# A new hand-written order for the first stage of a hybrid S5 and attention block, with more of its splitting on ScalarE and small S5 copies on GpSimd

## The chip, the cores and the metric

The kernel runs on one core of one Trainium2 chip. The metric is the device time of one execution in microseconds. Before the change the median of three runs is 1468.1 us (1466.05 to 1469.47).

## What is computed

One decoder block over a sequence of 1024 rows of width 1024, in float32. A vector `c` gives shifts and scales. The first stage of the kernel, which the change rewrites, makes the first shift and scale, the normed and modulated input `h`, its projection `u`, and the constants of the S5 recurrence:

```python
cond = jax.nn.silu(c)
mod = (cond @ w_ada[l] + b_ada[l])[:, None, :]
sh1, sc1, g1, sh2, sc2, g2 = jnp.split(mod, N_ADA, axis=-1)
h = modulate(rmsnorm(x, norm1_g[l]), sh1, sc1)      # h * (1 + scale) + shift
u, q, k, v, gate_a, gate_b = jnp.split(h @ w_in[l], IN_SPLITS, axis=-1)
...
lam_bar = jnp.exp(lam * dt)                          # per group and state
b_bar = ((lam_bar - 1.0) / lam)[..., None] * b
_, states = lax.associative_scan(_linear_recurrence, (a, bu), axis=1)
y = jnp.einsum('btgp,gip->btgi', states, cmat).real + d_skip * uf
```

The rest (stick-breaking attention, gates, output projection, SwiGLU) is not touched.

## The kernel before

Every float32 product is made of three products of shorter numbers. An operand is split in a high part (a copy that rounds, float32 to fp32r) and a low part (what is left), and TensorE multiplies high by high, low by high and high by low. So each `h` tile needs a high part and a low part before its products can run: tile `pa` or `pb`, `[:, 0]` high and `[:, 1]` low.

`start()` (from L560) is the first stage. It stands under a manual schedule: on all five engines its instructions run in the order in which the code issues them. What follows it (S5 proper, the value and gate projections, glu) is ordered by a scheduler that plays the program against a timeline of its own; so a change in `start()` also moves instructions behind it.

The stage, in its order:

- `x` comes in eight tiles of 128 rows, four for each half of the sequence (`load`). Each row gets its sum of squares (`squares`, tiles `sqa` on ScalarE and `sqv` on VectorE), then 1/rms (`rstd`, L481 to L487), and is scaled by it (`scale`, L637 and L639).
- `turn(h, k)` (L644) transposes 128 columns of the four scaled tiles of half `h` into a PSUM tile `tp`, of which there are two.
- `ada_products(g)` (L978, copied out at L611 into `acc`) and `ada_sums(g)` (L617) make shift and scale for 256 columns; VectorE finishes them as `mod` (L620) and `G` (L621).
- `modulate(h, k)` makes the split `h` tile: ScalarE writes the high part straight from PSUM (L648), VectorE computes the same value in float32 (`hf`, L650) and subtracts (L651).
- `product(h, ks, ms)` (L657) multiplies by `w_in`, split in `u_split` (L592, L593). There are 12 products of 512 columns for each `k` and half, 192 in all. `store(h, m)` (L661, L662) copies the sums out, on ScalarE for even `m` and on VectorE for odd `m`, and writes them to DRAM, from where the S5 stage reads them again as `u`.
- `S5.steps()` is a generator of the S5 constants, six pieces of small VectorE instructions (L85 to L168), which the stage calls between its own work. `S5.matrices()` (L185) ends the stage: `b_bar` (L73 to L78, `bbr` and `bbi`), twelve copies into `bst`, `A` and `B` (L202 to L207), eight transposes of `cl` on TensorE (L213) with two copies by ScalarE, and one of `dsk` (L217).

The order is: half 0 in four groups `g` of two `k` each (the last group of the first half is `g` = 3, tiles `u3h` and `u3l`), then half 1. The squares and scaling of half 1 stand in group 2, ahead of the copy L611 of group 3's sums. Each engine's instructions start in the order in which they stand.

Behind the stage VectorE builds the S5 matrices (`o<-C,A` L276, `scr<-Cs,B` L275, `e` L73 to L78 from copies L242 and L243 on ScalarE, `tc`/`tn`) while TensorE makes the values (L770) and gates (L749), whose weights need a low part from VectorE (`wl`, `wgl`, L455).

Of the kernel before, what the change touches and what calls it, by code (L numbers as in the profile page):

```python
# [9 lines left out]
F32 = mybir.dt.float32  # L10
# [18 lines left out]
class S5:  # L29
# [53 lines left out]
    def steps(self):  # L83
# [29 lines left out]
        for k in (11, 9, 7, 5, 3):  # L113
            stt(s, s, (-1) ** (k // 2) / math.factorial(k), w, ALU.add, ALU.mult)
        stt(s, s, 1.0, ph, ALU.add, ALU.mult)
        ts(c, w, -1.0 / math.factorial(14), None, ALU.mult)
        for k in (12, 10, 8, 6, 4, 2):
# [67 lines left out]
    def matrices(self):  # L185
        nc, pool, work = self.nc, self.pool, self.work
        v = nc.vector
        ts = v.tensor_scalar
        br, bi, zr, zi, lpr, lpi = self.br, self.bi, self.zr, self.zi, self.lpr, self.lpi
# [9 lines left out]
        for g in range(2):  # L199
            h = slice(64 * g, 64 * g + 64)  # L200
            lo, hi = slice(0, 64), slice(64, 128)
            v.tensor_copy(bst[lo, :, g], bbr[h])  # L202
            v.tensor_copy(bst[hi, :, g], bbi[h])
            v.tensor_copy(A[lo, :, g], lpr[h])
            ts(A[hi, :, g], lpr[h], -1.0, None, ALU.mult)
            ts(B[lo, :, g], lpi[h], -1.0, None, ALU.mult)
            ts(B[hi, :, g], lpi[h], -1.0, None, ALU.mult)  # L207
        self.C = pool.tile([128, 32, 16], F32, name="C")
# [8 lines left out]
        nc.tensor.transpose(ps[0:16, 0:32], self.dsk, self.ident[0:32, 0:32])  # L217
        nc.vector.tensor_copy(self.dT, ps[0:16, 0:32])

# [206 lines left out]
class Block:  # L426
# [132 lines left out]
    def start(self, const, up, s5p):  # L559
# [8 lines left out]
        with self.pool("s0", 1, side="right") as sp, self.pool("s0a", 1, side="right") as ap, self.pool("s5t", 1, side="right") as st, \  # L568
# [53 lines left out]

            def squares(h):
                for t in range(4 * h, 4 * h + 4):
                    if t % 2:
                        sq = ap.tile([P, 1024], F32, name="sqv")
                        nc.vector.scalar_tensor_tensor(sq, x[t], 1.0, x[t], ALU.mult, ALU.mult, accum_out=ss[:, t:t + 1])
                    else:
                        sq = ap.tile([P, 1024], F32, name="sqa")
                        nc.scalar.activation(sq, x[t], AF.Square, accum_out=ss[:, t:t + 1])  # L630

            def scale(h):
                r = self.rstd(const, ss[:, 4 * h:4 * h + 4], 4)
                for t in range(4):
                    xt, rt = x[4 * h + t], r[:, t:t + 1]
                    if t == 0:
                        nc.scalar.mul(xt, xt, rt)  # L637
                    else:
                        nc.vector.tensor_scalar(xt, xt, rt, None, ALU.mult)  # L639

# [5 lines left out]
            def modulate(h, k):  # L646
                t, q = self.hT[h][k], turned[h, k]
                nc.scalar.activation(t[:, 0], q, AF.Identity, bias=mod[:, 0, k:k + 1], scale=G[:, k:k + 1])  # L648
                f = ap.tile([P, 512], F32, name="hf", bufs=2)
                nc.vector.tensor_scalar(f, q, G[:, k:k + 1], mod[:, 0, k:k + 1], ALU.mult, ALU.add)  # L650
                nc.vector.tensor_tensor(t[:, 1], f, t[:, 0].bitcast(F32), ALU.subtract)  # L651
# [7 lines left out]
            def store(h, m):  # L659
                u = up.tile([P, 8, 64], F32, name="us", bufs=4)  # L660
                self.upin = (nc.vector.tensor_copy if m % 2 else nc.scalar.copy)(u, acc[m].rearrange("p (c j) -> p j c", j=8))  # L661
                nc.sync.dma_start(out=self.uD[P * m:P * m + P, :, 64 * h:64 * h + 64], in_=u)  # L662
# [8 lines left out]
            nc.vector.tensor_scalar(self.cond32, self.cond.unsqueeze(2).broadcast_to([P, KT, 32]), 1.0 / 32.0, None, ALU.mult)  # L671
            squares(0)
            scale(0)
            turn(0, 0)
# [6 lines left out]
            steps = s5.steps()  # L681
            next(steps)
            ada_sums(0)
            acc = [(self.mm, mp)[m // 2].tile([P, 512], F32, name="mm") for m in range(4)]
            for g in range(4):
                k = 2 * g
                modulate(0, k)
                modulate(0, k + 1)
                if g < 3:
                    u_split(g + 1)  # L690
                if g == 0:
                    u_load(2)
# [15 lines left out]
                next(steps)  # L708
                ada_sums(g + 1)
                product(0, (k + 1,), range(4))  # L710
            s5.load()
            self.hT[1] = [self.PB.tile([P, 2, 512], F32R, name="pb") for _ in range(KT)]
            product(0, (6,), range(4))
            turn(1, 0)
            modulate(1, 0)
            next(steps)
            for m in range(4):
                if m == 2:
                    turn(1, 1)
                    modulate(1, 1)  # L720
                product(0, (7,), (m,))
                store(0, m)
            acc = [xp.tile([P, 512], F32, name="mm")] + [(self.mm, self.mm, mp)[m].tile([P, 512], F32, name="mm") for m in range(3)]
            for k in range(4):
                turn(1, k + 2)
                product(1, (k,), range(4))
                modulate(1, k + 2)
                if k == 0:
                    next(steps)
            for k in (6, 7):  # L730
                turn(1, k)
                modulate(1, k)
            s5.matrices()
            for m in range(4):
                product(1, range(4, KT), (m,))
                store(1, m)


# [857 lines left out]
```

## Time and profile before

| | before |
|---|---|
| median of three runs | 1468.1 us |
| the profiled execution's own time | 1467.38 us |
| its span | 1465.7 us |
| TensorE busy | 1410.2 us, 96% |
| VectorE busy | 1091.1 us, 74% |
| ScalarE busy | 628.8 us, 43% |
| GpSimd busy | 511.6 us, 35% |

Some 1.7 us of the execution lie outside the span. A row of the timeline reads: start, duration, engine, line, operation, output <- input, and in brackets the idle time of the engine before it with what ended it. A row of the windows reads: the stretch, its length, then busy time and instructions of TensorE (PE), its weight loads, VectorE (DVE), ScalarE (ACT), GpSimd (POOL), the clock that TensorE was granted (1.00 is full), and the DMA share with GB/s. A busy TensorE need not be at its peak.

### The profile page before, as it was taken

What the parts mean: (1) busy time and instruction counts of PE and PEld (TensorE: products, weight loads), DVE (VectorE), ACT (ScalarE), POOL (GpSimd) and SP (SyncE); (2) the same over time, 40 slices, a digit from 0 to 9 for tenths busy, and PEclk for the clock granted to TensorE, in tenths of its full rate; (3) what the DMA queues carried; (4) which work ended last, traced back from release to release, by engine and by line L of the source; (5) the groups of instructions that cost most, each with busy time, mean ns of one, the idle gap of its engine ahead of it and who ended that gap; (6) DMA issues with size and microseconds to landing.
All of it is one profiled execution on the core that took longest, in us unless ns stands there. A gap on an engine that the chain in (4) does not pass through costs nothing.

```text
span 1465.7 us, 18286 instructions
## 1 busy us (share of the span) xinstructions
PE 1410.2 (96%) x6730; PEld 1117.0 (76%) x6730; DVE 1091.1 (74%) x1424; ACT 628.8 (43%) x829; POOL 511.6 (35%) x279
## 2 busy tenths in 40 slices
PE   5898999999899999999999999999999999999997
PEld 3678888788666666667888788888888888788886
DVE  5779996357788889886833679777766666889896
ACT  3321121642586858675418543223233323434334
POOL 1000000001211122102410014886757566689395
PEclk9999999999999999999999999999999999999999
DMA  9545664569211111116452223544434369899722
GB/s 338 142 108 160 155 179 117 180 214 343 89 44 43 37 51 58 51 51 216 143 201 87 86 87 101 182 146 166 148 120 147 122 204 370 293 376 369 246 85 115
DMA packets 193561, 233.39 MB, mean 159 GB/s; under 512 B 29500, under 2 KB 128896, under 8 KB 193472
## 3 DMA queue, kind: packets, MB, share of 16 engines
q1 hardware_dynamic: 184336, 224.70, 46.8%
q10 hardware_dynamic: 8912, 7.48, 1.9%
q8 instruction: 53, 0.87, 0.3%
q14 instruction: 36, 0.29, 0.1%
q0 software_dynamic: 224, 0.05, 0.0%
HBM read 162.85 MB, written 68.16 MB: 158 GB/s over the span
## 4 chain that ended last, share of the span: by engine, by line
PE 76%; DVE 10%; DMA 6%; ACT 5%; issue 2%; SPq 0%; POOL 0%; ACTq 0%; POOLq 0%; DVEq 0%
PE tq L1290 13%; PE wo L1290 6%; PE mm L1290 6%; PE tq L1411 6%; PE mx L823 5%; PE ga L749 4%; PE mm L823 4%; PE wo L1411 3%; PE mm L1411 3%; DMA aw<-in_w_ada_dram 2%; PE acc L823 2%; PE mm L1128 2%; PE mm L657 2%; PE z L823 2%; PE wo L1128 2%
## 5 line engine op out<-in xcount | busy, mean ns | idle before, releaser
L471 POOL TENSOR_TENSOR ws<-wb 128x1024 f32<-128x1024 f32 x24 | 61.6, 2567 | 175.4 <-DVE wl L474 148.7
L455 POOL TENSOR_TENSOR wl<-ws,wh 128x1024 fp32r<-128x1024 f32 x12 | 30.8, 2564 | 163.4 <-ACT wh L452 108.8
L916 DVE TENSOR_TENSOR wa<-wa,acc 128x512 f32<-128x512 f32 (+1 forms) x80 | 47.0, 628 | 32.6 <-ACT row L914 30.2
L294 POOL MEMSET tz<- 128x1024 f32 x4 | 3.8, 953 | 179.8 <-PE mm L657 96.7
L1337 POOL TENSOR_TENSOR pa<-pa 128x512 f32<-128x512 f32 x30 | 63.2, 2135 | 0.3
L1281 POOL TENSOR_TENSOR f<-f,f 128x512 f32<-128x512 f32 x30 | 53.2, 1797 | 24.9 <-DVE f L1275 19.6
L888 ACT ACTIVATE ws<-wa 128x1024 f32<-128x1024 f32 (+1 forms) x40 | 39.0, 976 | 48.6 <-DVE wa L885 48.3
L893 DVE TENSOR_TENSOR wl<-ws,wh 128x1024 fp32r<-128x1024 f32 (+1 forms) x40 | 57.1, 1427 | 1.0
L474 DVE TENSOR_TENSOR wl<-ws,wh 128x1024 fp32r<-128x1024 f32 x23 | 42.0, 1827 | 20.4 <-ACT wh L473 20.4
L993 DVE SCALAR_TENSOR_TENSOR acc<-aw,cond,acc 128x512 f32<-128x512 f32 x56 | 43.9, 784 | 7.0 <-DMA aw<-in_w_ada_dram 6.0
L1366 POOL TENSOR_TENSOR pa<-pa,row 128x1024 f32<-128x1024 f32 x14 | 43.7, 3135 | 14.9 <-DMA pa<-in_w_ffn_down_dram 14.9
L1411 PE MATMUL tq<-f,f 128*128 128x512 f32 x156 | 47.2, 390 | 1.3 <-DVE f L474 1.3
L1274 ACT ACTIVATE f<-f 128x1024 f32<-128x1024 f32 x20 | 21.2, 1061 | 62.1 <-DVE f L1310 31.4
L891 DVE SCALAR_TENSOR_TENSOR ws<-wa,ws 128x1024 f32<-128x1024 f32 (+1 forms) x40 | 45.5, 1136 | 2.9 <-ACT ws L890 1.9
L919 ACT ACTIVATE wa<-wa 128x1024 f32<-128x1024 f32 (+1 forms) x40 | 38.8, 971 | 19.5 <-DVE wa L916 18.5
L452 ACT CAST wh<-ws 128x1024 fp32r<-128x1024 f32 x24 | 25.0, 1049 | 48.6 <-PE wo L1128 23.3
L473 ACT CAST wh<-ws 128x1024 fp32r<-128x1024 f32 x23 | 24.1, 1053 | 50.6 <-PE tq L1290 31.1
L823 PE MATMUL z<-q,k 64*128 64x512 f32 (+3 forms) x192 | 41.8, 526 | 4.0 <-DVE wa L885 2.8
L1290 PE MATMUL tq<-pa,wh 128*128 128x512 f32 x144 | 44.3, 389 | 0.0
L1290 PE MATMUL tq<-x,wh 128*128 128x512 f32 x144 | 44.3, 389 | 0.0
L471 POOL TENSOR_TENSOR wgs<-wb 128x1024 f32<-128x1024 f32 x12 | 28.9, 2407 | 42.0 <-DVE wl L474 21.1
L473 ACT CAST wh<-wb 128x1024 fp32r<-128x1024 f32 x25 | 26.2, 1051 | 40.1 <-PE tq L1290 19.1
(914 smaller groups left out, 4687.0 us busy)
## 6 DMA issues: line engine op xcount, KB each, us to landing
wb<-hD SPq DMA_DIRECT2D x40, 512.0 KB, 6.0
aw<-in_w_ada_dram SPq DMA_DIRECT2D x64, 256.0 KB, 4.4
hD<-f SPq DMA_DIRECT2D x30, 512.0 KB, 5.5
ws<-in_w_in_dram SPq DMA_DIRECT2D x23, 512.0 KB, 4.4
wb<-in_w_ffn_gate_dram SPq DMA_DIRECT2D x44, 256.0 KB, 4.2
wb<-in_w_ffn_up_dram SPq DMA_DIRECT2D x44, 256.0 KB, 4.9
ws<-hD SPq DMA_DIRECT2D x20, 512.0 KB, 6.2
x<-in_x_dram SPq DMA_DIRECT2D x16, 512.0 KB, 7.1
```

Of the source, the lines that this page charges most:

```text
L471: (add or nc.gpsimd).tensor_tensor(st, a, b, op)
L473: nc.scalar.copy(h, a)
L749: self.nc.tensor.matmul(ps, lhsT=w[a][:, k], rhs=act[h][k][:, b], start=(j == 0), stop=(j == n - 1))
L823: return self.tc.keep_in_program_order(self.nc.tensor.matmul(*args, **kw))
L891: nc.vector.scalar_tensor_tensor(st, a, 0.0, st, ALU.max, ALU.add)
L893: nc.vector.tensor_tensor(lt, st, ht.bitcast(F32), ALU.subtract)
L916: nc.vector.tensor_tensor(a[:, x, 0:f], a[:, x, 0:f], r[:, x, 0:f], ALU.subtract)
L1128: self.nc.tensor.matmul(ps, lhsT=mg[t // 4][k][:, a, P * (t % 4):P * (t % 4) + P], rhs=ws[k // 2][b][:, k % 2], start=k + j == 0, stop=k + ...
L1281: self.last_sum = nc.gpsimd.tensor_tensor(o, a, b, op)
L1290: self.nc.tensor.matmul(ps, lhsT=w[x][:, q, k], rhs=self.B[i](y, k), start=(j == 0), stop=(j == 11))
L1337: self.after(nc.gpsimd.tensor_tensor(t[:, n], part(a), part(b), SIGN_B[i]), first)
L1411: nc.tensor.matmul(ps, lhsT=o[x][:, P * t:P * t + P], rhs=o[y][:, R], start=(j == 0), stop=(j == 3 * np_ - 1))
```

## The change

It rewrites the order of `start()` and moves work between engines; the arithmetic stays as it is.

- The squares and the scaling of half 1 are taken apart. Two squares of half 1, one on ScalarE and one on VectorE, now stand ahead of the copy of group 3's sums and two behind it, both on ScalarE; the scaling stands behind group 3's `modulate`.
- `modulate` has a second form, for odd `k` and all of half 1: ScalarE writes the float32 value `hf` from PSUM and then copies it to the high part from SBUF; VectorE only subtracts. Twelve `hf` instructions go from VectorE to ScalarE, and twelve copies of 128x512 are added on ScalarE.
- The S5 steps are cut in eight pieces and called later: the first behind group 0 and not ahead of `ada_sums(0)`, the polynomials for sine and cosine in half 1 and not in group 2.
- Half 1 takes its last two tiles in the loop (`k` up to 5), so only `k` = 6 and 7 are left for the end, where 24 and not 48 products stand.
- The twelve copies into `A`, `B` and `bst` go to GpSimd. The transposes of `cl` and `dsk` come behind the second of the last four products (`turned`); the copy `dT` goes to ScalarE.
- All four sums of half 1 are copied out by ScalarE.
- On the DMA queue the third and fourth `w_in` tiles are loaded behind `w_ada` tiles.

```diff
             def modulate(h, k):
                 t, q = self.hT[h][k], turned[h, k]
-                nc.scalar.activation(t[:, 0], q, AF.Identity, bias=mod[:, 0, k:k + 1], scale=G[:, k:k + 1])
                 f = ap.tile([P, 512], F32, name="hf", bufs=2)
-                nc.vector.tensor_scalar(f, q, G[:, k:k + 1], mod[:, 0, k:k + 1], ALU.mult, ALU.add)
+                if h == 0 and k % 2 == 0:
+                    nc.scalar.activation(t[:, 0], q, AF.Identity, bias=mod[:, 0, k:k + 1], scale=G[:, k:k + 1])
+                    nc.vector.tensor_scalar(f, q, G[:, k:k + 1], mod[:, 0, k:k + 1], ALU.mult, ALU.add)
+                else:
+                    nc.scalar.activation(f, q, AF.Identity, bias=mod[:, 0, k:k + 1], scale=G[:, k:k + 1])
+                    nc.scalar.copy(t[:, 0], f)
                 nc.vector.tensor_tensor(t[:, 1], f, t[:, 0].bitcast(F32), ALU.subtract)
...
-                self.upin = (nc.vector.tensor_copy if m % 2 else nc.scalar.copy)(u, acc[m].rearrange("p (c j) -> p j c", j=8))
+                self.upin = (nc.vector.tensor_copy if m % 2 > h else nc.scalar.copy)(u, acc[m].rearrange("p (c j) -> p j c", j=8))
...
                 if g == 0:
+                    ada_load(2)
                     u_load(2)
-                    ada_load(2)
-                    u_load(3)
                     load(1)
                 if g == 1:
                     ada_load(3)
-                if g == 2:
-                    squares(1)
-                    scale(1)
+                    u_load(3)
                 if g == 3:
                     break
+                if g == 2:
+                    square(4, True)
+                    square(5, False)
                 product(0, (k,), (0, 1))
                 ada_products(g + 1)
...
-                next(steps)
+                if g < 2:
+                    next(steps)
+                if g == 1:
+                    next(steps)
+                if g == 2:
+                    square(6, True)
+                    square(7, True)
+                    next(steps)
+                    r = self.rstd(const, ss[:, 4:8], 4)
                 ada_sums(g + 1)
                 product(0, (k + 1,), range(4))
+            for t in range(4, 8):
+                scale(r, t)
...
-            for k in range(4):
+            for k in range(6):
                 turn(1, k + 2)
                 product(1, (k,), range(4))
                 modulate(1, k + 2)
-                if k == 0:
+                if k < 3 or k == 5:
                     next(steps)
-            for k in (6, 7):
-                turn(1, k)
-                modulate(1, k)
             s5.matrices()
             for m in range(4):
-                product(1, range(4, KT), (m,))
+                product(1, (6, 7), (m,))
                 store(1, m)
+                if m == 1:
+                    s5.turned()
```

In `matrices` the twelve copies change their engine:

```diff
-            v.tensor_copy(bst[lo, :, g], bbr[h])
-            v.tensor_copy(bst[hi, :, g], bbi[h])
-            v.tensor_copy(A[lo, :, g], lpr[h])
...
+            gp.tensor_copy(A[lo, :, g], lpr[h])
+            gp.tensor_scalar(A[hi, :, g], lpr[h], -1.0, None, ALU.mult)
...
+            gp.tensor_copy(bst[lo, :, g], bbr[h])
+            gp.tensor_copy(bst[hi, :, g], bbi[h])
+
+    def turned(self):
```

On ScalarE, at the end of group 2, these rows stood before (`u3h` is the high part of the fourth weight tile, `sqa` a square, `acc` the copy that `ada_sums(3)` waits for, `pa` the high parts of group 3):

```order
L592 CAST u3h<-ws 128x1024
L630 ACTIVATE sqa,ss_108<-x 128x1024 x2
L482 ACTIVATE ry<-rv 128x4
L483 ACTIVATE ry<-ry 128x4
L637 ACTIVATE x<-x,ry 128x1024
L611 COPY acc<-mm 128x512
L648 ACTIVATE pa<-tp,mod_141,G_142 128x512 x2
```

At the same place on ScalarE now:

```order
L596 CAST u3h<-ws 128x1024
L630 ACTIVATE sqa,ss_108<-x 128x1024
L615 COPY acc<-mm 128x512
L630 ACTIVATE sqa,ss_108<-x 128x1024 x2
L486 ACTIVATE ry<-rv 128x4
L487 ACTIVATE ry<-ry 128x4
L649 ACTIVATE pa<-tp,mod_141,G_142 128x512
L652 ACTIVATE hf<-tp,mod_141,G_142 128x512
L653 CAST pa<-hf 128x512
L636 ACTIVATE x<-x,ry 128x1024
```

The copy `acc` has moved ahead of two squares, the 1/rms and the scaling, and the scaling has moved behind the high parts.

On VectorE, where half 0 ends and half 1 begins, these rows stood before (`rho` is the last of the long S5 step, `us` the copies of the sums of half 0, `pb` a low part of half 1):

```order
L147 TENSOR_TENSOR rho<-rho 128x16
L661 COPY us<-mm 128x512
L650 TENSOR_SCALAR hf<-tp,G_142,mod_141 128x512
L651 TENSOR_TENSOR pb<-hf,pb 128x512
L661 COPY us<-mm 128x512
L650 TENSOR_SCALAR hf<-tp,G_142,mod_141 128x512
L651 TENSOR_TENSOR pb<-hf,pb 128x512
```

At the same place on VectorE now (`sa` is the polynomial for the sine):

```order
L638 TENSOR_SCALAR x<-x,ry 128x1024 x3
L654 TENSOR_TENSOR pb<-hf,pb 128x512
L664 COPY us<-mm 128x512
L654 TENSOR_TENSOR pb<-hf,pb 128x512
L664 COPY us<-mm 128x512
L654 TENSOR_TENSOR pb<-hf,pb 128x512
L113 TENSOR_SCALAR sa<-aw 128x128
L115 SCALAR_TENSOR_TENSOR sa<-sa,aw 128x128 x5
```

The copies `us` now stand ahead of all S5 steps of this half, and no `hf` is left here.

On TensorE, at the end of the loop over half 1, these rows stood before (`tp` are transposes, `cl` and `dsk` S5 inputs):

```order
L657 MATMUL mm<-pb,wh 128x512
L644 MATMUL tp<-ident,x 128x128 x8
L213 MATMUL tp<-ident,cl 128x128 x8
L217 MATMUL tp<-ident,dsk 16x32
L657 MATMUL mm<-pb,wgh 128x512
L657 MATMUL mm<-pb,wgl 128x512
```

The same transposes on TensorE now (the rows of L781 are the first value products, which the scheduler puts here; the last 12 products of L660 follow later):

```order
L660 MATMUL mm<-pb,u3l 128x512
L660 MATMUL mm<-pb,u3h 128x512
L217 MATMUL tp<-ident,cl 128x128 x8
L781 MATMUL mm<-wh,pa 128x256
L781 MATMUL mm<-wl,pa 128x256
L781 MATMUL mm<-wh,pa 128x256 x2
```

The 17 transposes in a row are gone: two turns have moved into the loop, and those of `cl` stand behind products.

More of the change, by code (lines that the diff above doesn't have):

```diff
@@ L93, in steps @@
         self.vexp(r, ar, tmp)
+        yield
         def reduce(n, th):
@@ L115, in steps @@
         stt(s, s, 1.0, ph, ALU.add, ALU.mult)
+        yield
         ts(c, w, -1.0 / math.factorial(14), None, ALU.mult)
@@ L201, in matrices @@
             lo, hi = slice(0, 64), slice(64, 128)
[L202 to L207 removed]
+            gp.tensor_copy(A[lo, :, g], lpr[h])
+            gp.tensor_scalar(A[hi, :, g], lpr[h], -1.0, None, ALU.mult)
+            gp.tensor_scalar(B[lo, :, g], lpi[h], -1.0, None, ALU.mult)
+            gp.tensor_scalar(B[hi, :, g], lpi[h], -1.0, None, ALU.mult)
+            gp.tensor_copy(bst[lo, :, g], bbr[h])
+            gp.tensor_copy(bst[hi, :, g], bbi[h])
+    def turned(self):
+        nc, pool = self.nc, self.pool
         self.C = pool.tile([128, 32, 16], F32, name="C")
@@ L217, in matrices @@
         nc.tensor.transpose(ps[0:16, 0:32], self.dsk, self.ident[0:32, 0:32])
-        nc.vector.tensor_copy(self.dT, ps[0:16, 0:32])
+        nc.scalar.copy(self.dT, ps[0:16, 0:32])
     def phases(self):
@@ L621, in ada_sums, with square, scale @@
                 nc.vector.scalar_tensor_tensor(G[:, s], mod[:, 1, s], 1.0, self.cols[:, 48 + 2 * g:50 + 2 * g], ALU.add, ALU.mult)
[L623 to L639, printed above, removed]
+            def square(t, act):
+                sq = ap.tile([P, 1024], F32, name="sqa" if act else "sqv")
+                if act:
+                    nc.scalar.activation(sq, x[t], AF.Square, accum_out=ss[:, t:t + 1])
+                else:
+                    nc.vector.scalar_tensor_tensor(sq, x[t], 1.0, x[t], ALU.mult, ALU.mult, accum_out=ss[:, t:t + 1])
+            def scale(r, t):
+                if t % 4 == 0:
+                    nc.scalar.mul(x[t], x[t], r[:, t % 4:t % 4 + 1])
+                else:
+                    nc.vector.tensor_scalar(x[t], x[t], r[:, t % 4:t % 4 + 1], None, ALU.mult)
             def turn(h, k):
@@ L671, in start @@
             nc.vector.tensor_scalar(self.cond32, self.cond.unsqueeze(2).broadcast_to([P, KT, 32]), 1.0 / 32.0, None, ALU.mult)
-            squares(0)
-            scale(0)
+            acc = [(self.mm, mp)[m // 2].tile([P, 512], F32, name="mm") for m in range(4)]
+            for t in range(4):
+                square(t, t % 2 == 0)
+            r = self.rstd(const, ss[:, 0:4], 4)
+            for t in range(4):
+                scale(r, t)
             turn(0, 0)
@@ L681, in start @@
             steps = s5.steps()
-            next(steps)
             ada_sums(0)
-            acc = [(self.mm, mp)[m // 2].tile([P, 512], F32, name="mm") for m in range(4)]
             for g in range(4):
@@ L707, in start @@
                 turn(0, k + 3)
-                next(steps)
+                if g < 2:
[7 more added lines that the diff above has]
+                    r = self.rstd(const, ss[:, 4:8], 4)
                 ada_sums(g + 1)
                 product(0, (k + 1,), range(4))
+            for t in range(4, 8):
+                scale(r, t)
             s5.load()
@@ L713, in start @@
             product(0, (6,), range(4))
-            turn(1, 0)
-            modulate(1, 0)
-            next(steps)
             for m in range(4):
-                if m == 2:
-                    turn(1, 1)
-                    modulate(1, 1)
                 product(0, (7,), (m,))
                 store(0, m)
+                if m % 2 == 0:
+                    turn(1, m // 2)
+                    modulate(1, m // 2)
             acc = [xp.tile([P, 512], F32, name="mm")] + [(self.mm, self.mm, mp)[m].tile([P, 512], F32, name="mm") for m in range(3)]
-            for k in range(4):
+            for k in range(6):
                 turn(1, k + 2)
```

4 lines of the change are left out of this document (2 added, 2 removed).

## The prediction

> **What bounds the kernel now.** I read the page first, then the busy time of the engines in windows cut at the stage's own joints, then the timeline at each wait of TensorE.
>
> ```profile
> span 1465.7 us, 18286 instructions
> ...
> PE 1410.2 (96%) x6730; PEld 1117.0 (76%) x6730; DVE 1091.1 (74%) x1424; ACT 628.8 (43%) x829; POOL 511.6 (35%) x279
> ```
>
> TensorE is busy nearly throughout, but a busy TensorE includes slow stretches. The windows over the first stage, two stretches inside it, and the S5 stage behind it (length; PE, PEld, DVE, ACT, POOL busy; granted clock; DMA):
>
> ```profile
> 46.70:62.20 15.50, 11.39 (x73) 7.89 (x73) 13.26 (x35) 4.41 (x8) 0.00 (x0) 0.89 0.52 140
> 62.20:82.80 20.60, 18.39 (x93) 14.60 (x92) 16.84 (x59) 6.62 (x9) 0.00 (x0) 1.00 0.34 78
> 82.80:102.20 19.40, 16.47 (x68) 12.89 (x67) 10.40 (x27) 5.81 (x9) 0.00 (x0) 0.82 0.28 65
> 55.70:59.20 3.50, 3.30 (x9) 2.02 (x7) 2.74 (x12) 0.36 (x1) 0.00 (x0) 0.51 0.00 0
> 59.20:61.30 2.10, 0.79 (x3) 0.35 (x3) 1.61 (x3) 1.09 (x2) 0.00 (x0) 1.00 0.00 0
> 86.40:93.20 6.80, 6.12 (x19) 4.40 (x18) 6.62 (x21) 1.17 (x2) 0.00 (x0) 0.50 0.27 77
> 102.20:210.00 107.80, 101.63 (x750) 92.60 (x748) 99.70 (x232) 19.33 (x40) 3.07 (x6) 0.98 0.65 166
> ```
>
> Between 46.7 and 102.2 us TensorE waits, and twice it runs at half clock: 3.5 us from 55.7 and 6.8 us from 86.4. ScalarE is idle for two thirds of this time and VectorE is what TensorE mostly waits for. Here the waits are, with what ended each in brackets:
>
> ```profile
> 53.01 0.57 ACT L611 COPY acc<-mm 128x512 f32<-128x512 f32 x1
> 53.62 1.05 PE L617 MATMUL adap<-ones,acc 128*128 128x1 f32 x8 [2.61 <-ACT acc L611]
> ...
> 71.20 0.50 PE L657 MATMUL mm<-pb,wh 128*128 128x512 f32 x1 [1.88 <-DVE us L661]
> ...
> 82.77 1.03 PE L644 MATMUL tp<-ident,x 128*128 128x128 f32 x8
> ...
> 86.06 0.78 PE L213 MATMUL tp<-ident,cl 128*128 128x128 f32 x4 [2.25 <-DVE hf L650]
> ...
> 87.52 1.12 PE L213 MATMUL tp<-ident,cl 128*128 128x128 f32 x4 [0.68 <-ACT C L214]
> ```
>
> Each of the two half-clock stretches follows one of these waits by about 2 us or less. In the chain of work that ended last, the same product runs at two speeds:
>
> ```profile
> 33.26 4.22 PE mm L657 x18
> ...
> 41.31 0.44 PE tp L644 x4
> 41.74 0.80 PE adap L617 x8
> ...
> 88.78 13.37 PE mm L657 x48
> ```
>
> 18 products in 4.22 us are 0.234 us each; 48 in 13.37 us are 0.279 each. So TensorE bounds the stage only between its waits, and what can be gained is the waits and the slow products. From 102.2 to 210 us VectorE is busy for 99.7 of 107.8 us, so an early TensorE is worth something there only if VectorE is early too.
>
> **The change, part by part.** Up to 46.7 us I cost it at nothing: TensorE's order is unchanged, and an `hf` on VectorE gives way to 0.6 us of ScalarE there. The cover is TensorE's own queue of products in each group; if it were gone, the price would be below 1 us a group.
>
> *Group 3's start (T1).* These rows carry the walk:
>
> ```profile
> 44.36 1.05 ACT L592 CAST u3h<-ws 128x1024 fp32r<-128x1024 f32 x1
> ...
> 46.48 1.06 ACT L630 ACTIVATE sqa<-x 128x1024 f32<-128x1024 f32 x1
> 47.45 0.19 ACT L630 ACTIVATION_READ_ACCUMULATOR sqa<-x 128x1 f32 x1
> ...
> 48.54 0.66 PE L644 MATMUL tp<-ident,x 128*128 128x128 f32 x4
> ...
> 50.48 0.17 DVE L481 TENSOR_SCALAR rv<-ss 128x4 f32<-128x4 f32 x1
> ...
> 51.75 0.16 DVE L487 TENSOR_TENSOR ry<-ry,ra 128x4 f32<-128x4 f32 x1
> ...
> 58.40 0.15 DVE L620 TENSOR_TENSOR mod<-adap,cols 128x4 f32<-128x4 f32 x1
> ...
> 58.84 1.45 ACT L648 ACTIVATE pa<-tp,mod,G 128x512 fp32r<-128x512 f32 x2 [5.27 <-DVE G L621]
> ...
> 61.25 0.73 PE L657 MATMUL mm<-pa,u3h 128*128 128x512 f32 x2 [0.84 <-DVE pa L651]
> ```
>
> The added copies of 128x512 have no row in this stage. The same form stands in the glu stage:
>
> ```profile
> L1027 ACT CAST y2p<-sg x8: 611/620/625, 289.4 to 307.9; 128x512 fp32r<-128x512 f32 x8
> ```
>
> I take 0.62 us for each. ScalarE then starts `u3h` at 44.36 + 0.62 = 45.0 and ends it at 46.0; one square (1.06, and 0.19 to read its sum) ends at 47.2, before TensorE is done with the sums at 48.54. So the copy `acc` starts at 48.6 and not at 53.01, and the wait of 2.61 us goes, and with it, I take it, the half clock behind it. What is late next is the coefficients: two squares on ScalarE (2.3 us) end at 51.5, 1/rms takes 50.48 to 51.91, so 1.4 us, to 53.0, `mod` and `G` 0.44 us (58.40 to 58.84), and `pa` starts at 53.5 and not 58.84. TensorE comes there at 54.5: 48.54 plus two turns of four transposes (0.44 each), six products (1.4), the sums (0.8) and twelve products (2.8). Its first low part is ready 61.25 - 58.84 = 2.4 us behind `pa`, at 55.9 and not 61.25. That is 5.3 us earlier; T1 = 5.2, rounded down.
>
> *Start of half 1 (T2).* The wait of 1.88 us was for a copy `us` that stood on VectorE behind the long S5 step. It now stands ahead of it. T2 = 1.9.
>
> *End of half 1 (T3, T4).* From 82.77 to 88.78 are 6.0 us, in which 17 transposes ran, work for 1.9 us at 0.44 for four. The eight turns wait no more (two sit in the loop; `tp` is freed by ScalarE), and those of `cl` stand behind products. T3 = 6.0 - 1.9 = 4.1, say 4.0. The 48 products at 0.234 take 11.2 us and not 13.37 if no wait slows the clock: T4 = 2.1.
>
> Does VectorE keep up, now that two S5 pieces move into half 1? Rows for its load:
>
> ```profile
> L650 DVE TENSOR_SCALAR hf<-tp,G,mod 128x512 f32<-128x512 f32 x16 | 12.9, 806 | 6.1 <-ACT pa L648 3.6 <-ACT pb L648 2.5
> ...
> 53.95 0.22 DVE L112 TENSOR_SCALAR sa<-aw 128x128 f32<-128x128 f32 x1
> ...
> 58.25 0.23 DVE L119 TENSOR_SCALAR ca<-ca 128x128 f32<-128x128 f32 x1
> ...
> 90.10 0.28 DVE L202 COPY bst<-bbr 64x256 f32<-64x256 f32 x1
> ...
> 93.28 0.18 DVE L218 COPY dT<-tp 16x32 f32<-16x32 f32 x1
> ```
>
> It was busy 16.84 + 10.40 = 27.2 us from 62.2 to 102.2. Eight `hf` (6.4), the twelve copies and `dT` (90.10 to 93.46, 3.4) and a copy `us` (0.7) go; the polynomials (53.95 to 58.48, 4.5) come: 21.2 us. TensorE needs 40.0 - 1.9 - 4.0 - 2.1 = 32 us for the same stretch. The joint that matters is the sixth tile: ahead of its low part VectorE has about the work of 62.2 to 82.8 with six `hf` (4.8) out and the polynomials in, 16.84 - 4.8 + 4.5 = 16.5 us, against five rounds of TensorE of twelve products and a turn, 5 x 3.25 = 16.3 us. They are equal, though the last S5 step of that window now comes later. So I take off 0.3 us for new waits, up to 3 for the range (one tile late by 1 us and a slow clock behind it).
>
> *The GpSimd copies.* No small copy of GpSimd stands in the trace. Its nearest rows:
>
> ```profile
> L294 POOL MEMSET tz<- 128x1024 f32 x4 | 3.8, 953 | 179.8 <-PE mm L657 96.7
> ...
> L471 POOL TENSOR_TENSOR ws<-wb 128x1024 f32<-128x1024 f32 x24 | 61.6, 2567 | 175.4 <-DVE wl L474 148.7
> ```
>
> Four to seven times the elements take 0.95 and 2.57 us, so a copy costs between 0.13 and 2.57 us; I take 0.4, near the memset in elements. Four stand between `bbi` (done at 90.10 before, so about 85 with T1) and the second half of `A`, which `o<-C,A` on VectorE waits for, with all of the S5 work queued behind it: `A` is there at 86.6, at 95 by the upper end. The cover is that VectorE's next work but two needs the copies `e` of ScalarE, which stand behind the last `us`:
>
> ```profile
> 102.18 0.25 ACT L242 COPY e<-bbr 128x64 f32<-128x64 f32 x1 [0.35 <-PE mm L657]
> ...
> 104.97 0.22 DVE L74 TENSOR_TENSOR p<-e,lpi 128x64 f32<-128x64 f32 x1
> ...
> 140.92 0.48 PE L770 MATMUL mm<-wl,pa 128*128 128x256 f32 x1 [4.72 <-DVE wl L455]
> ```
>
> TensorE's last product of the stage comes at 102.2 - 13 = 89 us, or 91 with the value products that now run ahead of it; so `e` comes at 91, `p<-e` at 91.5, and 85 + 4p + 1.4 (two `o` of 0.7) is hidden up to p = 1.3 us a copy. The upper end costs 85 + 10.3 + 1.4 - 91.5 = 5 us. [...]
>
> *Behind the stage (T5).* VectorE and TensorE both enter the S5 stage some 13 us earlier, with the same work. The scheduler has reordered it: the two low parts of which TensorE awaited one for 4.72 us now stand ahead of the widest `tc` products and not behind them. New waits may come; I take 2 of the 4.7 us.
>
> The sum: 5.2 + 1.9 + 4.0 + 2.1 - 0.3 = 12.9 in the stage, 14.9 with T5. The profiled execution took 1467.38 us, 0.7 under the median of 1468.1. I predict 1467.4 - 14.9 = 1452.5.
>
> **The rivals.**
>
> *The lead is spent in the S5 stage.* `e` comes only 102.18 - 91.3 = 11 us earlier, and VectorE with its loads is the bound there (99.7 of 107.8 us). For it: the chain of waits runs over VectorE there. Against: VectorE's own load is not raised. If a late tile costs its 3 us as well and the new order loses 2 us, the gain is 13 - 3 - 2 - 1 = 7: 1460.
>
> *More goes than the waits of the stage.* If the whole 4.72 us goes and as much as 2 us of slow products behind it, the gain is 13 + 6.7: 1447.5.
>
> *GpSimd becomes the bound, slower than before.* If `A` comes so late that VectorE stands still, all S5 work moves. From 85 + 4p + 1.4 = 91.5 + 15 the gain is gone: p = 5.0 us. At p = 6 VectorE is 18.9 us late and the result is 1467.4 + 3.9 = 1471.3. Against: the widest row is 2.57 us for four times the elements.
>
> *The change does not do what it says:* the coefficients of group 3 or a late load hold TensorE as long as `acc` did, and VectorE is late in half 1 by what T2 to T4 give. Then 1467.
>
> *The clock.* A half clock of 3.5 us stood behind the wait of 2.61 us, none in the 2.1 us from 59.2, with two waits. The walk leaves TensorE one wait of about 1.3 us. [...]
>
> **How the numbers follow.** The forecast (1449 to 1457) gets 0.55, the lead spent (1457 to 1464) 0.20, more gone (1442 to 1449) 0.17, GpSimd as the bound 0.04, no effect 0.04. The likeliest is 1452.5. The range reaches over the first three but for their ends, with 3 us of late tile and clock and 5 us of GpSimd on one side and 6.7 us of S5 waits on the other: 1443 to 1462. A measurement of this kernel tells 0.2%, 2.9 us, from no change. Faster by more: 0.92; within: 0.04; slower: 0.04.
>
> **What would show it.** In the profile after: no wait for the copy `acc` in group 3 and `pa` of group 3 at 53 to 54.5 us; clock 1.00 in the stage from 30 us on; the products at 0.234 throughout; the last product of the stage at 88 to 92 us; `o<-C,A` at 86 to 89 us and the first `p<-e` at 91 to 93. It would be wrong if the low part of the sixth tile held TensorE, if small GpSimd copies took over 2 us each, or if TensorE's waits between 100 and 330 us grew by more than 4 us.

## The result, and the profile after

The changed kernel takes 1458.67 us (median of five runs, 1455.89 to 1462.33) against 1468.1. The ratio is 0.9942 with a 95% interval of 0.9921 to 0.9963, so it is 5.4 to 11.6 us faster (8.5 by the ratio, 9.4 by the medians); 14.9 were forecast. Its profiled execution is the longest of the five (1462.33 us) and only 5.1 us shorter than the profiled one of before (1467.38).

The page of the changed kernel:

```profile
span 1460.6 us, 18303 instructions
...
PE 1411.3 (97%) x6730; PEld 1117.7 (77%) x6730; DVE 1081.5 (74%) x1395; ACT 640.1 (44%) x846; POOL 514.7 (35%) x291
```

Its windows over the same places: group 3 with the start of half 1; from the start of group 3's products to the end of the stage, in two pieces; the S5 stage; and its four half-clock stretches ahead of 400 us:

```profile
46.70:62.20 15.50, 14.90 (x101) 11.34 (x100) 10.59 (x33) 9.85 (x18) 0.00 (x0) 1.00 0.58 150
...
56.10:74.90 18.80, 18.80 (x95) 15.52 (x96) 14.26 (x45) 10.84 (x16) 0.00 (x0) 1.00 0.38 85
74.90:91.60 16.70, 16.70 (x95) 14.17 (x94) 10.76 (x41) 8.29 (x14) 6.41 (x13) 1.00 0.39 97
23.30:30.20 6.90, 6.43 (x38) 2.81 (x38) 6.06 (x22) 2.06 (x3) 0.00 (x0) 0.51 1.09 352
91.60:199.40 107.80, 106.87 (x764) 96.33 (x763) 99.51 (x230) 21.55 (x42) 2.66 (x6) 1.00 0.66 175
238.35:241.80 3.45, 3.45 (x19) 3.45 (x18) 0.00 (x0) 0.66 (x2) 0.00 (x0) 0.51 1.09 309
269.00:275.90 6.90, 5.57 (x14) 4.19 (x14) 3.05 (x3) 6.09 (x7) 0.26 (x1) 0.51 0.37 115
368.00:374.90 6.90, 6.17 (x15) 4.13 (x16) 4.11 (x5) 4.22 (x5) 0.00 (x0) 0.51 0.02 4
```

From 56.1 us to the end of the stage TensorE is busy without a gap, at full clock. Ahead of 400 us there were four half-clock stretches before (at 55.7, 86.5, 141.1 and 284.4 us, 17 us in all) and there are four now (24 us in all); they have moved, three of them behind the stage. The timeline of the changed kernel at the steps of the prediction:

```profile
49.00 0.59 ACT L615 COPY acc<-mm 128x512 f32<-128x512 f32 x1 [1.56 <-PE mm L989]
...
51.18 0.95 PE L621 MATMUL adap<-ones,acc 128*128 128x1 f32 x8
...
53.66 0.78 ACT L649 ACTIVATE pa<-tp,mod,G 128x512 fp32r<-128x512 f32 x1 [1.16 <-DVE G L625]
...
56.06 0.73 PE L660 MATMUL mm<-pa,u3h 128*128 128x512 f32 x2 [0.60 <-DVE pa L654]
...
84.14 1.03 PE L217 MATMUL tp<-ident,cl 128*128 128x128 f32 x8
...
91.02 0.59 ACT L664 COPY us<-mm 128x512 f32<-128x512 f32 x1 [0.81 <-PE mm L660]
91.07 0.07 DVE L230 MEMSET tc<- 128x16 f32 x1 [4.20 <-PE mm L660]
...
91.11 0.76 DVE L280 TENSOR_TENSOR o<-C,A 128x576 f32<-128x576 f32 x1
...
93.05 0.21 DVE L74 TENSOR_TENSOR p<-e,lpi 128x64 f32<-128x64 f32 x1
```

So the stage did nearly what was forecast: the S5 chain starts with `p<-e` at 93.05 instead of 104.97. Most of the loss comes behind it. Of the kernel before, the last copy of the S5 results (`y`), the last gelu (the second of two in its row), and the first two groups of `z`, the scores with which attention begins:

```profile
253.74 0.59 ACT L353 COPY y<-s5a 128x512 f32<-128x512 f32 x1 [1.20 <-PE s5a L351]
...
280.49 2.08 ACT L1040 ACTIVATE y<-raw 128x512 f32<-128x512 f32 x2 [1.56 <-DMA raw<-yD]
...
371.56 0.93 PE L823 MATMUL z<-q,k 64*128 64x128 f32 x8 [1.19 <-DVE na L1076]
378.25 0.92 PE L823 MATMUL z<-q,k 64*128 64x384 f32 x4 [2.83 <-DVE wa L885]
```

The same of the changed kernel, with the DMA queues between (SPq and ACTq are the issuing queues; `yD` takes the S5 results out, `raw` reads them back for the gelu; `aD` stores a finished adaLN sum):

```profile
237.84 0.46 PE L354 MATMUL s5a<-u,tz 128*128 128x128 f32 x2 [4.81 <-DMA gD<-gst]
...
243.63 0.58 ACT L357 COPY y<-s5a 128x512 f32<-128x512 f32 x1
243.96 0.37 SPq L449 DMA_DIRECT2D wgs<-in_w_glu_dram  x1
244.25 5.42 ACTq L360 DMA_DIRECT2D yD<-y  x4
...
253.03 0.34 SPq L1050 DMA_DIRECT2D raw<-yD  x1
...
272.39 1.15 ACT L1051 ACTIVATE y<-raw 128x512 f32<-128x512 f32 x1 [0.29 <-DMA raw<-yD]
...
359.78 0.93 PE L834 MATMUL z<-q,k 64*128 64x128 f32 x8 [1.18 <-DVE na L1087]
...
362.48 0.33 SPq L1005 DMA_DIRECT2D aD<-acc  x1
...
365.19 1.86 DVE L950 TENSOR_SCALAR row<-ident 128x1024 fp32r<-128x1024 f32 x2 [2.74 <-DMA aD<-acc]
...
368.73 1.65 PE L834 MATMUL z<-q,k 64*128 64x384 f32 x4 [5.07 <-DVE wa L896]
```

The lead over before is 10.1 us at the last `y`, 9.1 at the last gelu (281.4 before), 11.8 at the first `z`, and 9.5 at the second group. There TensorE waits 5.07 us and not 2.83: it waits for VectorE (`wa`), and VectorE's `row`, ahead of it, waits until the store `aD` of the last adaLN sum has landed. The two share no data, so I read this as memory that the store still holds. Over the half-clock stretch behind it the lead falls by another 2.6 us, to 6.9 at the 101st `z` product.

### The profile page after: what moved, and what is told of

It is laid out like the page before. It is cut to its first block, busy times and chain, and to the rows that moved or that the text cites. A ratio compares the mean times of both kernels' runs of the same rounds, so it can differ in the third digit from the quotient of the medians.

```text
span 1460.6 us, 18303 instructions
## 1 busy us (share of the span) xinstructions
PE 1411.3 (97%) x6730; PEld 1117.7 (77%) x6730; DVE 1081.5 (74%) x1395; ACT 640.1 (44%) x846; POOL 514.7 (35%) x291
## 4 chain that ended last, share of the span: by engine, by line
PE 74%; DVE 8%; issue 5%; DMA 5%; ACT 4%; POOL 3%; SPq 1%; POOLq 0%; DVEq 0%; ACTq 0%
PE tq L1301 10%; PE tq L1422 6%; PE mx L834 5%; PE wo L1301 5%; PE mm L1301 5%; PE mm L834 5%; PE ga L760 4%; PE mm L760 3%; PE wo L1422 3%; PE mm L660 3%; PE mm L1422 3%; PE acc L834 2%; PE mm L1139 2%; PE z L834 2%; PE mx L760 2%
## 5 line engine op out<-in xcount | busy, mean ns | idle before, releaser
L458 POOL TENSOR_SCALAR wh<-ws 128x1024 fp32r<-128x1024 f32 x6 | 7.4, 1239 | 105.2 <-issue 36.1
```

## The experiments

Ratios are to the kernel before on the same chip. The table gives, for the profiled execution of a run, how many microseconds earlier than in before (first column) an instruction starts, from unrounded times; the last row is the whole execution. Each column is one execution: the two of the changed kernel differ by up to 3.5 us in a row, so differences of that size between columns prove nothing. Between S5 and attention lie `glu`, with its products `ga` on TensorE, and `branch_a`, which ends in the products `na` on VectorE. A chunk is one of the eight sums of `c` with 512 columns of `w_ada` (adaLN, numbers 4 to 11) that VectorE makes beside them, four in S5 and four in `branch_a`; each is stored in `aD`.

| | before | after | after, again | group 3 alone | half 1 alone | load behind | chunk early | load and chunk |
|---|---|---|---|---|---|---|---|---|
| last `us` of the stage | 103.0 | 12.0 | 11.3 | 3.8 | 8.5 | 12.5 | 11.9 | 12.2 |
| last `y` of S5 | 253.7 | 10.1 | 8.3 | 2.5 | 6.2 | 9.9 | 9.2 | 9.7 |
| last gelu | 281.4 | 9.1 | 7.0 | 4.3 | 7.0 | 9.7 | 6.9 | 9.0 |
| first `z` | 371.6 | 11.8 | 10.9 | 6.6 | 9.8 | 16.5 | 8.7 | 13.0 |
| second group of `z` | 378.3 | 9.5 | 11.1 | 6.8 | 8.1 | 11.7 | 9.3 | 12.9 |
| 101st `z` product | 508.1 | 6.9 | 9.7 | 5.4 | 8.2 | 8.5 | 9.3 | 13.0 |
| execution | 1467.38 | 5.1 | 8.6 | 7.6 | 7.6 | 8.5 | 11.0 | 14.0 |

### The same kernel again

> The changed kernel itself, as a common base on one chip for the three runs that go with it. 1456 to 1461 by both theories. In its profile theory A (the stage's lead of about 13 us is in hand where ga begins) wants the first ga product at 263 to 267 us again and TensorE's longest wait between 225 and 240 us at about 5 us, since it comes of the order and not of the execution.

1460.57 us against 1467.41; ratio 0.9959 (0.9940 to 0.9978), twelve runs. First `ga` at 266.6, the wait near 238 us 4.9. So the wait near 238 us comes back in the second profiled execution; the wait where attention begins was only 2.56 us this time, less than before the change, though `row` waited for the same store again.

### The parts of the stage

Group 3 alone (in the kernel before):

```diff
+                if g == 3:
+                    scale(1, r1)
+                    break
                 if g == 2:
-                    squares(1)
-                    scale(1)
-                if g == 3:
-                    break
+                    squares(1, (4, 5))
...
+                if g == 2:
+                    squares(1, (6, 7), (6, 7))
                 next(steps)
+                if g == 2:
+                    r1 = self.rstd(const, ss[:, 4:8], 4)
                 ada_sums(g + 1)
```

> The kernel before with the new order of group 3 alone: two squares of half 1 ahead of the copy of the sums, two behind it on ScalarE, the scaling behind group 3's modulate; everything else as before. Theory A (a lead of the stage reaches the end, less a bounded loss where attention begins): T1 gives its 5.2 us in the stage, and the time is 1462 to 1465. Theory B (S5 and glu set the time, and a lead of TensorE alone is spent there, or half 1 waits for VectorE that much longer): 1466.5 to 1469.

1461.91 us; ratio 0.9956 (0.9936 to 0.9976), 6.5 us by the ratio (3.5 to 9.4). Theory A's side in time. But the stage ends only 3.8 us earlier, not 5.2: the wait of 2.61 us for `acc` is gone here, and yet TensorE falls to half clock, later, behind a wait of 1.43 us for `pa` (56.31):

```profile
57.40:60.80 3.40, 2.92 (x7) 2.37 (x8) 3.37 (x6) 0.56 (x1) 0.00 (x0) 0.50 0.00 0
```

Half 1 alone (in the changed kernel, the squares, 1/rms and scaling of half 1 back ahead of the copy `acc`):

```diff
                 if g == 2:
-                    square(4, True)
-                    square(5, False)
+                    for t in range(4, 8):
+                        square(t, t % 2 == 0)
+                    r = self.rstd(const, ss[:, 4:8], 4)
+                    for t in range(4, 8):
+                        scale(r, t)
...
```

> The changed kernel with group 3 in its old order: all four squares of half 1, the 1/rms and the scaling ahead of the copy of group 3's sums. Theory A (parts of the stage add up, and what they give reaches ga): T1 is lost, so the last product of the stage comes 4 to 6 us later than in the changed kernel and the time is 1462 to 1465. Theory B (S5 and glu set the time and TensorE's lead alone is worth nothing): 1457 to 1460.

1459.00 us; ratio 0.9944 (0.9924 to 0.9963): as much as the changed kernel gains, without T1. Theory A is wrong here as stated. The stage does end 3.5 us later than in the changed kernel (table), but at the last gelu the run is level with that kernel's second profile. Parts that give 6.5 and 8.2 us alone give 6.0 and 8.5 in the two measurements together.

The high parts back on the old split (in `modulate`, `if True:` for `if h == 0 and k % 2 == 0:`):

> The changed kernel with the old form of modulate for every tile: the high part from PSUM on ScalarE and hf on VectorE, so that twelve hf of 0.8 us go back to VectorE and twelve copies of 0.62 us leave ScalarE. Theory A: VectorE is level with TensorE in half 1 (16.5 against 16.3 us by the prediction), so eight hf more make it late by 4 to 6 us there: 1461 to 1465. Theory B: VectorE has slack in half 1, and the order alone made the gain: 1457 to 1459.5.

1466.75 us; ratio 0.9980 (0.9959 to 1.0001). Both theories missed: most of the gain goes, more than theory A had. TensorE of this run waits, ahead of the last transposes of half 1, until the `hf` of the sixth tile has freed their PSUM tile, so VectorE is late, as theory A has it, and the last `us` comes at 96.55. That is still 6.5 us earlier than before; at the last gelu 2.0 us of it are left. Why the rest goes behind the stage was not tested:

```profile
82.30 1.09 PE L643 MATMUL tp<-ident,x 128*128 128x128 f32 x4 [3.54 <-DVE hf L650]
```

The copies back on VectorE (`v, gp = nc.vector, nc.vector` in `matrices`):

> The changed kernel with the twelve small copies of matrices back on VectorE. Theory A: on GpSimd they took 0.3 to 0.65 us each and were hidden; on VectorE they stand in the S5 chain for about 3 us (90.10 to 93.46 us in the profile of before), and since that chain sets the start of ga, the time is 1460.5 to 1463. Theory B (the S5 chain is not what carries the lead, or GpSimd slows VectorE by as much as it takes from it): 1457.5 to 1459.5.

1460.03 us; ratio 0.9929 (0.9909 to 0.9949). Between the two bounds, and not to be told from the changed kernel. `p<-e` comes 1.8 us later (94.88), but not for the copies: they stand at 87.17 to 90.33 us, and VectorE still waits behind them, for 1.13 and not 4.20 us:

```profile
91.46 0.07 DVE L230 MEMSET tc<- 128x16 f32 x1 [1.13 <-PE mm L660]
```

The copies of the changed kernel, as groups by shape (count, busy, mean ns):

```profile
L206 POOL TENSOR_SCALAR B<-lpi 64x144 f32<-64x144 f32 x2 | 1.2, 614 | 0.1
...
L207 POOL COPY bst<-bbr 64x256 f32<-64x256 f32 x2 | 0.9, 460 | 6.6 <-DVE bbr L77 6.6
...
L203 POOL COPY A<-lpr 64x144 f32<-64x144 f32 x2 | 0.6, 320 | 72.1 <-DVE lpr L77 72.0
```

They took 0.32 to 0.61 us, and VectorE stood idle for 4.20 us ahead of its first S5 work in any case: the `tc` that it writes there waits for the stage's last product, with which it shares no data, only, as I read it, memory.

### Behind the stage: S5 and glu

One adaLN chunk out of S5 (`if m < 3:` ahead of `self.ada_rest(4 + m, ap, self.upin)`, and `self.ada_rest(7, tp, gelu, 2)` behind the gelus of `glu`):

> The changed kernel with the fourth of the adaLN chunks that stand in the S5 stage (chunk 7: eight multiply-adds of 0.75 us on VectorE, 6 us, and eight loads) taken out of S5 and into the glu stage, where VectorE is busy for 15.9 of 45 us. Theory C: behind the stage VectorE's S5 chain sets when ga begins; TensorE's products of the gates are only a filler, so a wait of TensorE that is removed there (the 4.72 us for wl) comes back as another (4.81 us at 237.84) as soon as the filler is used up. Then 6 us less on VectorE bring the first ga forward by 3 to 6 us, to 260 to 263, and the time is 1453 to 1456. Theory D: TensorE's amount of work between the stage and ga, or the loads, set it; then ga stays at 264 to 266 and the time at 1457 to 1460.

1459.61 us; ratio 0.9952 (0.9935 to 0.9969). Theory D's time, and theory C's mechanism only in part: with the chunk gone, the last `y` comes 2.2 us earlier than in the changed kernel (241.41) and the first `ga` at 263.8, between the two theories. The last gelu starts at 267.73, 4.7 us earlier than in the changed kernel, but part of that has another cause: here the stores `yD` stand ahead of the second `w_glu` load, and 5.8 and not 9.4 us pass from the last `y` to the first `raw`. The chunk's loads left S5 with its multiply-adds; the two were not taken apart. The chunk has only moved, and it is paid for further on. The run's last gelu and what TensorE waits for behind it:

```profile
267.73 1.21 ACT L1051 ACTIVATE y<-raw 128x512 f32<-128x512 f32 x1 [0.55 <-DMA raw<-yD]
```

```profile
288.38 0.73 PE L760 MATMUL ga<-yp,wgh 128*128 128x512 f32 x2 [2.33 <-ACT sg L1065]
...
360.62 0.93 PE L834 MATMUL z<-q,k 64*128 64x128 f32 x8 [2.87 <-DVE na L1088]
368.00 0.92 PE L834 MATMUL z<-q,k 64*128 64x384 f32 x4 [3.49 <-DVE wa L896]
```

The same move in the kernel before:

> The kernel before with the same chunk 7 moved from S5 to the glu stage and nothing else. There TensorE waits 4.72 us for wl and then only 2.31 us where ga begins (283.69 us). Theory C (VectorE's S5 chain sets the start of ga before the change too): the first ga comes 3 to 6 us earlier than 279 us and the time is 1463 to 1466. Theory D (before the change TensorE is as late as the chain, so a shorter chain alone gives little): 1467 to 1469.5.

1473.23 us; ratio 1.0052 (1.0035 to 1.0069): slower, which neither theory had. The last gelu starts 4.3 us earlier there too (277.1), but the first `z` comes at 373.7 and not 371.6: an early `ga` was worth nothing there, as attention did not begin early too. These 2.2 us are less than the 5.1 to 10.1 us that the run is slower; the rest was not traced to a cause.

The second `w_glu` load behind the first gelu. In the changed kernel this 512 KB load stands ahead of the stores `yD` (243.96, above): from the last `y` to the first `raw` pass 253.03 - 243.63 = 9.4 us (7.8 in the second profile). With half 1 alone it stands behind them, and 6.0 us pass:

```profile
247.56 0.59 ACT L357 COPY y<-s5a 128x512 f32<-128x512 f32 x1 [0.38 <-PE s5a L355]
...
248.18 1.89 ACTq L360 DMA_DIRECT2D yD<-y  x4
250.56 1.10 SPq L449 DMA_DIRECT2D wgs<-in_w_glu_dram  x1
...
253.58 0.82 SPq L1048 DMA_DIRECT2D raw<-yD  x2
```

```diff
+                if m + j == 0:
+                    self.gelu = g
...
-            w = self.w3(self.weight(src[:, :, 256 * c:256 * c + 256]), 256)
+            w = self.w3(self.weight(src[:, :, 256 * c:256 * c + 256], first=self.gelu if c else None), 256)
```

> The changed kernel with one load moved: the second w_glu tile (512 KB, issued at 243.93 us in the profile of after, ahead of the last stores yD) now waits for the first gelu. Theory E: group 3 and half 1 do not add up (5.5 us alone, 8.5 alone, 7 to 9 together) because with both the scheduler puts this load ahead of the last yD stores on the DMA queue; these then need 8.8 us from the last copy y to the first read raw, 5.5 us in the run with half 1 alone. Then here they need 5 to 6 us again, the last gelu starts at 269 to 271 us instead of 272.4 to 274.5, and the time is 1455 to 1458. Theory F: ScalarE or the reads raw themselves set the gelu chain, or what is won is waited for behind it: the time stays at 1458.5 to 1461.

1459.65 us; ratio 0.9940 (0.9922 to 0.9957): theory F's time. From the last `y` (243.83) to the first `raw` 6.7 us pass and the last gelu starts at 271.7: both earlier than in the changed kernel, but by less than theory E had. The run's timeline shows where it went:

```profile
244.44 3.32 ACTq L360 DMA_DIRECT2D yD<-y  x4
...
250.55 0.34 SPq L1050 DMA_DIRECT2D raw<-yD  x1
...
355.07 0.93 PE L834 MATMUL z<-q,k 64*128 64x128 f32 x8 [0.84 <-DVE na L1089]
360.86 0.33 SPq L1005 DMA_DIRECT2D aD<-acc  x1
...
366.54 1.01 PE L834 MATMUL z<-q,k 64*128 64x384 f32 x2 [7.58 <-DVE wa L896]
```

TensorE comes to attention 4.7 us earlier than in the changed kernel and then waits 7.58 us, since `row` waits for the store of the last adaLN sum again (2.15 us). Only 0.7 of the 4.7 us are there at the last gelu. In part the rest is the clock: the changed kernel ran at half clock for 6.9 us from 269.0 (above), this one not:

```profile
266.00:278.00 12.00, 10.89 (x47) 8.27 (x46) 4.19 (x5) 10.03 (x12) 2.40 (x1) 1.00 0.47 156
```

The two q/k weight loads behind it as well (`self.qk_proj(0, qp, kp, self.gelu)`):

> As the run with the w_glu load behind, and the two q/k weight loads (512 KB each, issued at 249.13 and 249.62 us between the stores yD and the reads raw) behind the first gelu as well. Theory E: the first raw comes another 1 to 2 us earlier and the last gelu at 267 to 270 us: 1453.5 to 1457. Theory F: 1458.5 to 1461; if the q/k weights come late for the qx products (298.6 us), 1 to 3 us worse.

1460.35 us; ratio 0.9944 (0.9925 to 0.9962), theory F's time; the last gelu at 273.1 (theory E had 267 to 270), the first `z` at 356.1, and the wait is 7.6 us again.

The single load in the kernel before:

> The kernel before with the same second w_glu load behind the first gelu. There the load (250.56 us, 7.46 us to landing in the chain of waits) also stands ahead of the stores yD. Theory E: 2 to 3 us from the gelu chain, 1464 to 1466.5. Theory F: 1466.5 to 1469.

1467.84 us; ratio 1.0001 (0.9984 to 1.0018): nothing, by theory F. The last gelu did not come earlier (282.7). The expectation had named the wrong load: the one at 250.56 is the first `w_glu` load, and the second was issued at 258.72, behind the stores `yD` already. So this run says nothing on a load ahead of the stores.

### Where attention begins

Chunk 8 into the glu stage:

```diff
+        self.ada_rest(8, tp, gelu, 2)
...
-            for n in ((8, 9), (10,), (11,), ())[c]:
+            for n in ((9,), (10,), (11,), ())[c]:
```

> The changed kernel, with one of the four late chunks of the adaLN sums (chunk 8 of w_ada, eight multiply-adds on VectorE and their loads) taken out of branch_a and into the glu stage, so that VectorE's last multiply-add of branch_a stands ahead of nine products na and not behind all of them. Theory A: the stage's 13 us are still there when ga begins (283.69 us before, 270.56 after); about half is lost where attention begins, because the last chunk's store (issued at 362.48 us) holds the memory that the first instructions of attention need. TensorE then waits 5.07 us (2.83 before) and runs 6.8 us at half clock behind it. Then here the wait is at most 3 us, the clock stays full, and the time is 1453 to 1456. Theory B: the lead is lost in the S5 and glu stages and the entry to attention is an effect of it: then nothing changes, 1457.5 to 1460; the chunk's loads among the reads of the glu stage may even make it 2 us worse.

1458.83 us; ratio 0.9933 (0.9909 to 0.9957). By time theory B; by the trace the wait is 2.18 us with no half clock behind it, as theory A has it, but TensorE comes to the first `z` only at 362.9, 3.1 us later than in the changed kernel; 2.1 of these are there at the last gelu already. So, by the traces, either edit alone brings one of two chains forward, and the other one holds. Both together:

> The changed kernel with both edits at once: the second w_glu load behind the first gelu, and chunk 8 of the adaLN sums in the glu stage. With the load alone TensorE came to attention (first z) at 355.1 us, 4.7 us earlier than in the changed kernel, and waited 7.58 us there for the store of the last adaLN chunk (issued 360.86); with the chunk alone the store was early, but TensorE came at 362.9 us. Theory G (where attention begins, two chains meet, TensorE's and the adaLN chunks' of branch_a, so that a lead counts only when both have it): here both have it, the second group of z starts at 360 to 363 us instead of 366.5 to 368.9, and the time is 1453.5 to 1457. Theory H (the traffic of glu and branch_a as a whole, weights, gates, chunks and products, sets the start of attention, so that a chunk moved forward makes branch_a's products wait): the second group of z stays at 365 to 369 us and the time at 1458 to 1461.

1455.87 us; ratio 0.9916 (0.9894 to 0.9939), the lowest ratio here; its interval does not meet that of the changed kernel's second measurement (0.9940 to 0.9978), but overlaps with the first (0.9921 to 0.9963) and with those of the two single edits (0.9922 to 0.9957 and 0.9909 to 0.9957). So the times don't show that the two edits are worth more together than their sum; that rests on the traces. The time is theory G's. The second group of `z` comes at 365.33, later than G's 360 to 363 and inside H's bounds:

```profile
358.52 0.93 PE L834 MATMUL z<-q,k 64*128 64x128 f32 x8 [0.84 <-DVE na L1090]
361.52 1.45 DVE L950 TENSOR_SCALAR row<-ident 128x1024 fp32r<-128x1024 f32 x2 [3.05 <-DMA nD<-na]
365.33 0.92 PE L834 MATMUL z<-q,k 64*128 64x384 f32 x4 [2.94 <-DVE wa L896]
```

Now `row` waits 3.05 us for a store of the products `na` (`nD`) and no longer for that of the adaLN sum, and no half clock follows TensorE's wait of 2.94 us. The lead of the stage, 12.2 us, is whole at the 101st `z` product (13.0). Between 100 and 400 us this execution has 3.4 us at half clock, the changed kernel's two have 17 and 14.

## Why the prediction was right or wrong

- **T1, right in group 3.** The copy `acc` at 49.00 (48.6 forecast), `pa` at 53.66 (53.5), the first low part used at 56.06 and not 61.25: 5.2 us, as taken. TensorE's one wait there is 0.60 us. No half clock from 30.2 us to the stage's end. At the end of the stage it was worth less: 3.8 us with group 3 alone, 3.5 when it is taken out.
- **Up to 46.7 us, right.** Here nothing was charged. The changed kernel has a new half-clock stretch at 23.3 us, but the run with one chunk out of S5 has none there, and its last `us` comes at 90.88 instead of 91.02:

```profile
23.30:30.20 6.90, 5.34 (x39) 2.65 (x40) 5.48 (x18) 3.01 (x4) 0.00 (x0) 1.00 1.09 353
```

- **T2 to T4, nearly right in size.** No wait and no slow product in half 1; the last product ends at 91.0 (91 forecast with the value products ahead of it). All in all the stage ends 12.0 us earlier (11.3 in the second profile), and 12.9 were forecast. That VectorE is only just level with TensorE was right too: with `hf` back TensorE waits 3.54 us.
- **GpSimd, right.** The copies lie near the 0.4 us taken and stay hidden. What hides them was named wrongly: `o<-C,A` came at 91.11, not at 86 to 89, for want of the stage's memory, as I read the wait of 4.20 us ahead of it, and in the run with the copies on VectorE they were hidden there as well. `p<-e` at 93.05 is at the end of the forecast's 91 to 93. The runs with the copies on either engine differ by less than their intervals (0.9942, 0.9921 to 0.9963, on GpSimd; 0.9929, 0.9909 to 0.9949, on VectorE).
- **T5, the step that failed**, and with it the sentence that VectorE and TensorE enter S5 some 13 us earlier "with the same work". It counted on 2 us less of TensorE's waits behind the stage. The wait of 4.72 us for `wl` did fall, to 0.61 us at 122.01, but 4.81 us of waiting came at 237.84, and the sum of the waits stayed. Before, and in the changed kernel:

```profile
100.00:330.00 230.00, 221.42 (x1337) 191.72 (x1336) 166.68 (x330) 67.98 (x103) 8.91 (x10) 0.99 0.61 168
...
100.00:330.00 230.00, 221.19 (x1282) 188.66 (x1281) 166.32 (x310) 69.64 (x101) 8.01 (x9) 0.98 0.60 173
```

TensorE stands idle for 8.58 us of this stretch before and for 8.81 after. Its lead is 12.0 us at the end of the stage and 11.8 at the first `z` (11.3 and 10.9 in the second profile): T5 was +2 and came to about 0. The likely reason is that TensorE's products there only fill the time until VectorE's S5 chain is ready, and the filler was used up sooner; the run with a chunk out of S5 supports this in part only. The sign named for it, waits that grow by more than 4 us, did not show, since the sum did not grow.

- **Where attention begins: a loss that no term held.** In the first profile the lead falls from 11.8 us at the first `z` to 9.5 at the second group (the wait of 5.07 us), 6.9 at the 101st product (half clock) and 5.1 at the end; in the second from 10.9 to 11.1, 9.7 and 8.6. So 6.7 us went in one execution and 2.3 in the other. The sum put this at nothing without a reason. How much of it the new order causes and how much is the spread of executions stays open: the wait for the store stands in both profiles, its length differs.
- **The rival "the lead is spent in the S5 stage"** gave 1460, nearest to what was measured, and its band (1457 to 1464, chance 0.20) holds the result; the forecast's (1449 to 1457, 0.55) doesn't. Its number is partly luck. Of its terms the 3 us of a late tile did not occur. Its place holds for the gelus, which come 9.1 us earlier and not 12, but TensorE has made this up at the first `z`.
- **The clock.** T1 and T4 counted on no half clock behind the one wait of about 1.3 us that the walk left. That was the author's estimate, and as a rule it is doubtful: group 3 alone has a half clock behind a wait of 1.43 us, and in the changed kernel the one at 269.0 us stands behind two waits, of 0.97 us at 266.8 and 0.77 us at 268.0. The 3 us that the range held for a late tile and a slow clock no run shows as such: the stretch in group 3 alone lasted 3.4 us, and in the changed kernel's stage TensorE's wait was 0.60 us and the clock 1.00 from 30.2 us on.
- **The range** held 1458.67, and so did the direction. The measured gain is below the forecast by more than its interval: 11.6 at most against 14.9. A slip that changes nothing: a gain of 13 + 6.7 gives 1447.7, not 1447.5.

What stays open: why the parts of the stage do not add up. With half 1 alone the stage ends 3.5 us later than with all, yet the times are alike. The load ahead of `yD` (3.4 us more between `y` and `raw` in the first profile) and the wait at attention may account for it, but were not separated in that kernel, and each interval is some 3 us wide on either side.

## What to carry to other kernels

A lead in one stage is worth what is left of it at the next place where several chains meet, so follow it there by name, instruction by instruction, before adding it up; a wait of the busiest engine that is taken away can come back as another (here 4.72 us fell to 0.61 and 4.81 us came, I take it because the work in between is filler). Memory handed from one stage to the next can, as I read it, make such a meeting place: here VectorE's `row`, among the first tiles of the new stage, waited 2.74 us for the last small store of the old one. Where two chains meet, an edit that helps one of them can measure as little (1458.83 and 1459.65 us against 1455.87 with both), so try both together; whether they then give more than their sum takes narrower intervals than these.

## What the runs showed of the hardware

- The half clock came in stretches of 3.4 or 6.8 us (one of 10.2, with both loads behind, at 362.9 us; the last stretch of each execution, at its end, aside), and behind waits of 2.2 to 3.5 us one came in some places and none in others. Waits of 2.83 us (before, 378.25), 2.94 (load and chunk, 365.33) and 3.49 (chunk out of S5, 368.00) had none right behind them; 2.25 us (before, 86.06) had 6.8 us, 2.61 us (before, 53.62) had 3.4 us, and 2.56 us in the second profile of the changed kernel had 3.4 us at 368.6. The wait of 5.07 had 6.8, and so had the two of 0.97 and 0.77 us close together. What decides it was not shown.
- Executions of one kernel spread by more than the effects sought: before took 1462.48 to 1474.16 us in twenty runs on one chip, with a mean granted clock of 0.990 in the shortest and 0.983 in the longest.
